# Level products of a gated recurrence: one fp32 matmul per product against three fp32r matmuls on rounded halves, with half of the tokens moving

## The chip, the cores and the metric

The kernel runs on one core of a Trainium2 chip. The metric is the device time of one execution in microseconds, as the median of the runs shown. TensorE (PE in the profile) multiplies, and its weight loads have records of their own (PEld); VectorE is DVE, ScalarE is ACT, GpSimd is POOL, and SP issues most of the DMAs.

## The reference, cut to what matters

Two blocks of two layers each work on 256 tokens of width 2048. Nearly all of the arithmetic is in the projections. The change is in the first layer of the first block, in a gated recurrence with 8 heads of 128 channels:

```python
def hgrn2_chunkwise(q, logf, k, v):
    ...
    bcum = jnp.cumsum(lc, axis=3)
    causal = jnp.tril(jnp.ones((B_CHUNK, B_CHUNK), dtype=bool))
    pair = jnp.exp(jnp.minimum(bcum[:, :, :, :, None, :] - bcum[:, :, :, None, :, :], 0.0))
    att = jnp.einsum('bhnik,bhnjk,bhnijk->bhnij', qc, kc, pair)
    att = jnp.where(causal, att, 0.0)
    o_intra = jnp.einsum('bhnij,bhnjv->bhniv', att, vc)
    ...
    o = o_intra + o_inter
```

Over the whole sequence this is an attention matrix between tokens i and j <= i: the sum over the 128 channels of q_i * k_j * exp(sum of logf from j+1 to i), times v.

## The kernel before

**Projections.** Weights come from HBM as `raw` tiles of 128x1024 floats (SP issues the loads, line 205). ACT rounds a tile to `whi` (fp32r, `split_hi`, line 217) and DVE makes the rest `wlo = raw - whi` (`split_lo`, line 235). A product of activations and weights is then three fp32r matmuls, high by high, high by low, low by high, into one PSUM tile `ps` (`mm_step`, line 1234). A pair of one raw tile's halves is a piece; there are 804 pieces, up to 5 `whi` and 4 `wlo` tiles are alive at once, and each engine takes its instructions in the order in which they are written.

A piece of a chunk in mode "x" is 12 matmuls with 512 moving columns of weights and the activations as stationary operand; in mode "w" it is 24 matmuls with 256 moving columns of tokens and the weights stationary.

**Work between the pieces.** After each piece `pump` takes one step of the first generator in `pri` and one of the first three in `bg`, and `ahead` writes the splits of later pieces. So what a generator writes between two `yield`s comes to stand between two pieces on every engine.

**The levels.** `levels(hf)` (line 726) handles 4 heads, and runs twice. It builds the attention matrix by levels: at level l (0 to 6) the 256 tokens are cut into blocks of 2m tokens with m = 2^l, and each later half of a block meets the earlier half of the same block. `expo(l)` makes exp factors on ACT, one instruction for the later halves, one for the earlier. `factors(l, E)` updates the running sums `S` and `fb` and multiplies q into the later halves and k into the earlier halves of `E`, four DVE instructions. `products(l, E)` multiplies, for each head and each of the two blocks b of 128 tokens, the 128 columns of `E` by themselves (`mm`, recorded as line 133) into a PSUM bank `lv`, one bank for each b, and DVE copies the entries that a mask in `cl` selects into the matrix `Ad[b]` (line 768). Level 7 multiplies the first 128 tokens by the second 128, 4 products, and ACT copies them to `Ax`. In one loop turn `expo(l)` stands in one step, `factors(l)` and `products(l-1)` in the next, so two pieces of the projections lie between one level's products and the next.

The tiles `E` (128x1024) come from a pool of 11 pages, in which q, k and the running sums also live.

Of the kernel before, what the change touches and what calls it, by code (L numbers as in the profile page):

```python
# [10 lines left out]
F32 = mybir.dt.float32  # L11
# [14 lines left out]

# persistent constants
C_ID, C_ONE, C_GTT, C_LT, C_LE, C_LET, C_COS, C_SIN = 0, 128, 256, 384, 512, 640, 768, 832
C_W = 896
# constants of the even layer, then of the two modulated layers  # L30
L_W = 1024
# [68 lines left out]
def two_stacks_kernel(ctx: ExitStack, tc: tile.TileContext, A, out, layers="EODM"):  # L100
# [25 lines left out]
    def bank(n="bk"):  # L126
        return p_pb.tile([128, 512], F32, tag="b", name=n)
# [4 lines left out]
    def mm(o, l, r, start=True, stop=True, **k):  # L132
        PE.matmul(o, l, r, start=start, stop=stop, skip_group_check=True, **k)  # L133
# [20 lines left out]

    # ------------------------------------------------------------------ persistent data
    x = p_c.tile([128, 2, D], F32, name="x")
# [36 lines left out]

    # ------------------------------------------------------------------ weight stream
    units = deque()     # split / mod units in order
    raws = deque()      # raw loads in order, not yet issued
    live_raw = [0]
# [53 lines left out]

    # ------------------------------------------------------------------ modulation
    mod_acc = {}
# [14 lines left out]
    def mod_fin(key):  # L268
        """column sums of the partial products, plus the bias, to a row in DRAM"""
        (i, p), col = key  # L270
        acc = mod_acc.pop(key)
        c0 = p * D + col * 512
        r = t2("mrow")
        G.dma_start(r[0:1, :], A["mod_b_2"][i, c0:c0 + 512].unsqueeze(0))
        nw = None
        if p == 1:
            nw = t2("mnw")
            G.dma_start(nw[0:1, :], A["norm_w_2"][i, col * 512:(col + 1) * 512].unsqueeze(0))
        hi, lo = t2("mhi", F32R), t2("mlo", F32R)
        yield  # L280
        act(hi, acc, AF.Copy)
        yield
        V.tensor_sub(lo, acc, hi.bitcast(F32))
        yield
        yield
        bk = bank("mb")
        mm(bk[0:1, :], cr[:, 0:1], hi, stop=False)
        mm(bk[0:1, :], cr[:, 0:1], lo, start=False)
        tt(r[0:1, :], r[0:1, :], bk[0:1, :], ADD)
        if p == 1:  # L290
            yield
            stt(r[0:1, :], r[0:1, :], 1.0, nw[0:1, :], ADD, MUL)
        if col == 0:
            mod_row[i, p] = p_dr.tile([D], F32, name=f"mod{i}{p}")
        G.dma_start(mod_row[i, p][col * 512:(col + 1) * 512].unsqueeze(0), r[0:1, :])
# [14 lines left out]

    # ------------------------------------------------------------------ silu
    def silu_gen(ps, dst, after=None):
# [19 lines left out]

    # ------------------------------------------------------------------ norm at a layer's start
    class Norm:
# [80 lines left out]

    # ------------------------------------------------------------------ y^T
    yt = [Act()]
# [22 lines left out]
    def yS_gen(pg, q, gate=None):  # L440
        """split of a page [feat, 4 K-chunks, tok]"""
        Y = yt[0]
        yield
        while gate is not None and not gate():
            yield
        Y.hi[q] = hi = act32r("yhi")
        lo = act32r("ylo")
        src = pg.rearrange("p (k t) -> p k t", k=4)
        act(hi, src, AF.Copy)
        yield  # L450
        V.tensor_sub(lo, src, hi.bitcast(F32))
        Y.lo[q] = lo

    # ------------------------------------------------------------------ evacuations
    def v3(ps):
        return ps.rearrange("p (b f) -> p b f", b=2)

    def ev_T(ps, scale, dst):
        """[feat, head, tok] of 4 heads"""
        t = page("qkT")  # L460
        act(t, ps, AF.Copy, scale=scale)
        dst.append(t.rearrange("p (h t) -> p h t", h=4))
        yield
# [20 lines left out]

    # ------------------------------------------------------------------ layer E
    def layer_E():
# [8 lines left out]
        lbt = ms[:, 280:288]  # L495
        colA = ms[:, 288:296]      # log max(lb, floor)
        colC = ms[:, 296:304]      # log1p(-lb)
        colCA = ms[:, 304:312]
        col1 = ms[:, 312:320]      # 1 - lb
        colk = ms[:, 320:328]      # lb - max(lb, floor)  # L500
        cos = cp[:, C_COS:C_COS + 64].rearrange("p (b f) -> p b f", b=2)
# [11 lines left out]
        def prepare():  # L513
            for k, (w, sc) in enumerate([(qw, 0.125), (kw, 1.0)]):
# [8 lines left out]
                tabs.append((Ct, St))  # L523
            # softmax over the single even row, then cumsum minus the first row
            tt(lb, lbt, lbt, SUB)
# [13 lines left out]
        def rope(src, H, tab, outp):  # L539
            """src: PSUM view [128, 2, H*64]; writes outp [128, 2, H, 64] (normed, rotated)."""  # L540
            Ct, St = tab
# [134 lines left out]

        # ---- B
        def ev_f(ps, hf):
# [47 lines left out]
        def levels(hf):  # L726
# [33 lines left out]

            def products(l, E):
                if l < 7:
                    for b in range(2):
                        bk = bank("lv")
                        w = slice(b * 128, (b + 1) * 128)
                        for h in range(4):
                            mm(bk[:, h * 128:(h + 1) * 128], h4(E)[:, h, w], h4(E)[:, h, w])
                        V.copy_predicated(
                            h4(Ad[b]),
                            cl[:, None, l * 128:(l + 1) * 128].bitcast(I32).to_broadcast([128, 4, 128]), h4(bk))  # L770
                else:
                    bk = bank("lv")
                    for h in range(4):
                        mm(bk[:, h * 128:(h + 1) * 128], h4(E)[:, h, 0:128], h4(E)[:, h, 128:256])
                    act(Ax, bk, AF.Copy)
# [5 lines left out]
            yield  # L781
            for l in range(1, 8):
                En = expo(l)
                yield
                factors(l, En)
                products(l - 1, E)
                E = En
                yield
            del En
            yield  # L790
            products(7, E)
            del E, Sp, Pp, q, k
            while ("bi", hf) not in st:
# [48 lines left out]

    # ------------------------------------------------------------------ layer O
    def layer_O():
# [78 lines left out]

    # ------------------------------------------------------------------ layers D and M
    def layer_DM(which):
# [14 lines left out]
        def head(st, tri, g, h):  # L940
# [3 lines left out]
            g_ = g if which == "D" else 3  # L944
            dm = cl_h[0][:, g_ * 256:g_ * 256 + 256]     # the second block of queries; its right half is also the first
            sp = bank("s")
# [5 lines left out]
            yield  # L952
            m = sm("mD")       # 0:2 -max, 2:4 sums, 4:6 alpha, 8:10 -max so far, 10:12 denominator so far
            V.tensor_reduce(m[:, 0:1], s[:, 0:128], axis=AX.X, op=MAX, negate=True)
# [100 lines left out]

    # ------------------------------------------------------------------ plan
    def out_chunks(w, gate, nxt):
# [63 lines left out]
    def make_pieces(c, order=(0, 1, 2, 3)):  # L1121
        """raw loads and pieces of a chunk; the quarters of K in the given order"""
        wv = c.w.rearrange("(k p) n -> p k n", p=128)
        rk = 2 if c.n == 512 else 4
        for q in order:
            for r0 in range(q * 4, q * 4 + 4, rk):
                r = Raw("w", wv[:, r0:r0 + rk, c.c0:c.c0 + c.n], rk, c.n)
                r.left = 1
                c.pieces.append(Piece(r, 0, rk, c.n, r0))
        c.k_first, c.k_last = c.pieces[0].kc0, c.pieces[-1].kc0 + c.pieces[-1].nk - 1  # L1130
        return c.pieces
# [14 lines left out]
    with tc.manual_schedule():  # L1146
# [7 lines left out]

        # the plan of all layers: chunks in order, with the modulation matvec spread between
        plans = []
        norms = [norm_of[l]() for l in layers] + [norm_of["F"]()]
        for li, l in enumerate(layers):
# [7 lines left out]
            ws += po[0][:6] + po[1][:6] + po[0][6:] + po[1][6:] + po[2] + po[3] + po[4]  # L1166
            # the modulation's loads, spread evenly over a stretch of the layer
            w0, w1 = (len(ws) - 68, len(ws) - 12) if l == "E" else (16, len(ws) - 40)
# [39 lines left out]
        def norm_x(b):  # L1208
            """of the first layer: 1/rms on the diagonal of a matrix that transposes x"""
            for c0 in range(0, D, 512):  # L1210
                norm.squares(b, c0, 512)
            norm.rstd(b)
            d = t2("diag")[:, 0:128]
            ts(d, ident, norm.r[b], None, MUL)
            return d
# [49 lines left out]
        for li, (l, ch, setup, oc, po) in enumerate(plans):  # L1265
# [55 lines left out]

            # ---- output projection
            final[0] = li == len(plans) - 1
# [83 lines left out]
```

## Time and profile before

| | us |
|---|---|
| median of the 3 runs | 2548.24 (2547.06 to 2548.41) |
| profiled execution, from its first to its last instruction | 2546.2 |
| PE busy in it | 2511.9 |
| DVE busy | 1708.4 |
| ACT busy | 1225.4 |

The page gives the profiled execution's own time as its span; the timed median is 2.0 us above it, which is what lies around a span. Busy times of one engine count an instruction from its start to its end, with overlaps counted once. A matmul's record begins where it starts and ends some way behind the start of the next, because matmuls are pipelined: what one costs is read from the distance of starts or from the chain of work, not from its duration. An fp32 matmul leaves two records (and two weight loads), an fp32r matmul one.

### The profile page before, as it was taken

Reading aid. Unit: us, or ns where it says so; the run is one execution under the profiler, and the core shown is the slowest. Engines: PE = TensorE matmul, PEld = TensorE weight load, DVE = VectorE, ACT = ScalarE, POOL = GpSimd, SP = SyncE. Lnnn points to the kernel's source line nnn. Section 1 sums busy time; section 2 is a strip of 40 time slices with the busy share of each in tenths; the row PEclk is TensorE's granted clock in tenths of the full one; section 3 lists DMA queues with packets and bytes.
Section 4 is the critical chain, followed back from the end, with each engine's and each line's share of the span. In section 5 each row is a group of like instructions: output and inputs, shape, how many; then the busy total and the mean of one; then the engine's idle time right before and its main releaser. Section 6 shows DMA issues by size and latency. Waiting matters only on the chain.

```text
span 2546.2 us, 42808 instructions
## 1 busy us (share of the span) xinstructions
PE 2511.9 (99%) x17140; PEld 2334.2 (92%) x17140; DVE 1708.4 (67%) x2423; ACT 1225.4 (48%) x1747; POOL 86.7 (3%) x134
## 2 busy tenths in 40 slices
PE   7999999999999999999999999999999999999998
PEld 7898888999999989999999999989998899999987
DVE  5687866588888655566666666676566656676565
ACT  5555554454554544444444444444444444444443
POOL 1000200000000000000000000000000010000000
PEclk9999999999999999999999999999999999999999
DMA  7645435588878656666666676667666656766763
GB/s 233 182 134 172 151 131 190 167 269 286 270 267 281 207 167 202 222 229 225 228 224 220 222 239 219 220 225 238 221 225 203 204 159 220 240 214 221 232 202 110
DMA packets 293496, 539.36 MB, mean 212 GB/s; under 512 B 18784, under 2 KB 49664, under 8 KB 293296
## 3 DMA queue, kind: packets, MB, share of 16 engines
q1 hardware_dynamic: 288720, 527.97, 63.4%
q0 software_dynamic: 4576, 8.66, 1.4%
q8 instruction: 134, 2.20, 0.3%
q14 instruction: 66, 0.54, 0.1%
HBM read 534.41 MB, written 2.15 MB: 211 GB/s over the span
## 4 chain that ended last, share of the span: by engine, by line
PE 97%; DVE 1%; issue 1%; ACT 1%; DMA 0%; POOL 0%; POOLq 0%; ACTq 0%; DVEq 0%
PE ps L133 88%; PE oD L133 2%; PE s L133 2%; PE lv L133 1%; PE pT L136 1%; PE mb L133 0%; PE z L133 0%; PE oO L133 0%; PE oA L133 0%; DVE wlo L235 0%; PE rc L133 0%; PE hT L133 0%; DVE hlo L414 0%; ACT junk L139 0%; PE hT L136 0%
## 5 line engine op out<-in xcount | busy, mean ns | idle before, releaser
L235 DVE TENSOR_TENSOR wlo<-raw,whi 128x1024 fp32r<-128x1024 f32 x804 | 985.7, 1227 | 558.8 <-PE ps L133 281.4
L139 ACT ACTIVATE whi<-raw 128x1024 fp32r<-128x1024 f32 x804 | 849.3, 1059 | 951.1 <-PE ps L133 838.8
L133 PE MATMUL ps<-hhi,whi 128*128 128x256 f32 x3328 | 949.4, 285 | 0.0
L133 PE MATMUL ps<-hhi,wlo 128*128 128x256 f32 x3328 | 941.6, 283 | 0.0
L133 PE MATMUL ps<-hlo,whi 128*128 128x256 f32 x3328 | 941.5, 283 | 0.0
L133 PEld LDWEIGHTS ps<-hhi,whi 128*128 128x128 f32 x3328 | 638.3, 192 | 2.1 <-issue 1.4
L133 PEld LDWEIGHTS ps<-hlo,whi 128*128 128x128 f32 x3328 | 638.4, 192 | 1.2
L133 PEld LDWEIGHTS ps<-hhi,wlo 128*128 128x128 f32 x3328 | 638.1, 192 | 0.0
L133 PE MATMUL ps<-whi,hhi 128*128 128x512 f32 (+1 forms) x1152 | 437.1, 379 | 0.0
L133 PE MATMUL ps<-whi,hlo 128*128 128x512 f32 (+1 forms) x1152 | 427.8, 371 | 1.4 <-DVE hlo L414 1.1
L133 PE MATMUL ps<-wlo,hhi 128*128 128x512 f32 (+1 forms) x1152 | 426.2, 370 | 0.1
L151 DVE SCALAR_TENSOR_TENSOR macc<-raw,cs,macc 128x512 f32<-128x512 f32 x360 | 268.2, 745 | 0.6
L133 PEld LDWEIGHTS ps<-whi,hlo 128*128 128x128 f32 x1152 | 218.0, 189 | 40.8 <-DVE hlo L414 3.2
L133 PEld LDWEIGHTS ps<-whi,hhi 128*128 128x128 f32 x1152 | 218.5, 190 | 35.0 <-issue 1.1
L133 PEld LDWEIGHTS ps<-wlo,hhi 128*128 128x128 f32 x1152 | 218.6, 190 | 34.3 <-DVE wlo L235 0.3
L133 PE MATMUL ps<-whi,yhi 128*128 128x512 f32 (+1 forms) x640 | 224.5, 351 | 2.1 <-DVE gx L142 1.0
L133 PE MATMUL ps<-whi,ylo 128*128 128x512 f32 (+1 forms) x640 | 222.1, 347 | 0.0
L133 PE MATMUL ps<-wlo,yhi 128*128 128x512 f32 (+1 forms) x640 | 221.9, 347 | 0.0
L133 PEld LDWEIGHTS ps<-whi,yhi 128*128 128x128 f32 x640 | 121.2, 189 | 17.4 <-DVE gx L142 1.4
L133 PEld LDWEIGHTS ps<-whi,ylo 128*128 128x128 f32 x640 | 121.1, 189 | 15.2
L133 PEld LDWEIGHTS ps<-wlo,yhi 128*128 128x128 f32 x640 | 121.2, 189 | 14.7
L151 DVE SCALAR_TENSOR_TENSOR sD<-cld,s 128x128 f32<-128x128 f32 (+1 forms) x128 | 39.5, 350 | 55.2 <-PE s L133 54.1
(216 smaller groups left out, 1575.2 us busy)
## 6 DMA issues: line engine op xcount, KB each, us to landing
raw<-in_a_w_in_dram SPq DMA_DIRECT2D x320, 512.0 KB, 3.7
raw<-in_mod_w_dram SPq DMA_DIRECT2D x192, 512.0 KB, 4.5
raw<-in_w_in_odd_dram SPq DMA_DIRECT2D x128, 512.0 KB, 4.0
raw<-in_b_w_in_dram SPq DMA_DIRECT2D x128, 512.0 KB, 3.9
raw<-in_w_in_even_dram SPq DMA_DIRECT2D x100, 512.0 KB, 4.1
raw<-in_w_out_even_dram SPq DMA_DIRECT2D x32, 512.0 KB, 4.4
raw<-in_w_out_odd_dram SPq DMA_DIRECT2D x32, 512.0 KB, 4.3
raw<-in_a_w_out_dram SPq DMA_DIRECT2D x32, 512.0 KB, 4.6
```

The lines of the kernel that those rows point to most:

```text
L133: PE.matmul(o, l, r, start=start, stop=stop, skip_group_check=True, **k)
L136: PE.transpose(o, i, ident)
L139: S.activation(o, i, f, **k)
L151: V.scalar_tensor_tensor(o, a, s, b, op0=op0, op1=op1)
L235: V.tensor_sub(u.lo, u.raw.t[:, u.k0 * u.n:(u.k0 + u.nk) * u.n], u.hi.bitcast(F32))
```

## The change

The products are no longer fp32. `halves(E)` makes a rounded page `Eh` (ACT) and the rest `El = E - Eh` (DVE), both fp32r. `three` multiplies high by high, high by low and low by high into the same columns of PSUM. For levels 0 to 6 only the later half of each block moves (64 columns of the 128, with steps of 2m), since the mask lets nothing else through; the results of both b lie in one bank, and the masked copy takes 256 instead of 512 columns for each b. Level 7 keeps its 128 moving columns and becomes three matmuls too. Comments were dropped elsewhere in the file, and nothing else differs.

```diff
-            def products(l, E):
+            def halves(E):
+                Eh = p_pg.tile([128, 1024], F32R, tag="pg", name="Eh")
+                act(Eh, E, AF.Copy)
+                El = p_pg.tile([128, 1024], F32R, tag="pg", name="El")
+                V.tensor_sub(El, E, Eh.bitcast(F32))
+                return h4(Eh), h4(El)
+
+            def three(o, hi, lo, h, w, sel):
+                mm(o, hi[:, h, w], sel(hi), stop=False)
+                mm(o, hi[:, h, w], sel(lo), start=False, stop=False)
+                mm(o, lo[:, h, w], sel(hi), start=False)
+
+            def products(l, E2):
+                hi, lo = E2
                 if l < 7:
+                    m = 1 << l
+                    bk = bank("lv")
+                    second = lambda a: a.rearrange("p (n z m) -> p n z m", z=2, m=m)[:, :, 1, :]
                     for b in range(2):
-                        bk = bank("lv")
                         w = slice(b * 128, (b + 1) * 128)
                         for h in range(4):
-                            mm(bk[:, h * 128:(h + 1) * 128], h4(E)[:, h, w], h4(E)[:, h, w])
+                            o = bk[:, (b * 4 + h) * 64:(b * 4 + h + 1) * 64]
+                            three(o.rearrange("p (n m) -> p n m", m=m), hi, lo, h, w, lambda a: second(a[:, h, w]))
+                    for b in range(2):
                         V.copy_predicated(
-                            h4(Ad[b]),
-                            cl[:, None, l * 128:(l + 1) * 128].bitcast(I32).to_broadcast([128, 4, 128]), h4(bk))
+                            Ad[b].rearrange("p (h n z m) -> p h n z m", h=4, z=2, m=m)[:, :, :, 1, :],
+                            second(cl[:, l * 128:(l + 1) * 128].bitcast(I32))[:, None].to_broadcast([128, 4, 64 // m, m]),
+                            bk[:, b * 256:b * 256 + 256].rearrange("p (h n m) -> p h n m", h=4, m=m))
                 else:
                     bk = bank("lv")
                     for h in range(4):
-                        mm(bk[:, h * 128:(h + 1) * 128], h4(E)[:, h, 0:128], h4(E)[:, h, 128:256])
+                        three(bk[:, h * 128:(h + 1) * 128], hi, lo, h, slice(0, 128), lambda a: a[:, h, 128:256])
                     act(Ax, bk, AF.Copy)
...
             for l in range(1, 8):
+                E2 = halves(E)
+                del E
                 En = expo(l)
                 yield
                 factors(l, En)
-                products(l - 1, E)
+                products(l - 1, E2)
                 E = En
+                del En, E2
                 yield
-            del En
-            yield
-            products(7, E)
-            del E, Sp, Pp, q, k
+            E2 = halves(E)
+            del E
+            yield
+            products(7, E2)
+            del E2, Sp, Pp, q, k
```

On PE, before, a level's products stand as 8 fp32 matmuls between two pieces; here the first level of the first half of the heads.

```order
 L133 MATMUL ps<-wlo,hhi 128x512
 L133 MATMUL ps<-whi,hlo 128x512
-L133 MATMUL lv<-E 128x128 x8
-L133 MATMUL ps<-whi,hhi 128x512
-L133 MATMUL ps<-wlo,hhi 128x512
```

On PE, after, at the same place: `Eh` and `El` are the two rounded halves of `E`. Two products are shown, of the eight.

```order
+L133 MATMUL lv<-Eh 128x64
+L133 MATMUL lv<-El,Eh 128x64
+L133 MATMUL lv<-Eh,El 128x64
+L133 MATMUL lv<-Eh 128x64
+L133 MATMUL lv<-El,Eh 128x64
+L133 MATMUL lv<-Eh,El 128x64
```

The place between the pieces stays; what was 8 instructions is 24 with half of the moving columns.

On DVE, one level's stretch with its differences, at level 1 of the first half of the heads: `A_1091` and `A_1092` are the matrices of the two blocks of tokens.

```order
-L235 TENSOR_TENSOR wlo<-raw,whi 128x1024 x2
+L235 TENSOR_TENSOR wlo<-raw,whi 128x1024
+L766 TENSOR_TENSOR El<-E,Eh 128x1024
+L235 TENSOR_TENSOR wlo<-raw,whi 128x1024
 L142 TENSOR_TENSOR S<-S,fb 128x128x4
 L142 TENSOR_TENSOR fb<-fb 128x128x4
 L142 TENSOR_TENSOR E<-E,bq 128x128x4
 L142 TENSOR_TENSOR E<-E,fn 128x128x4
-L768 COPY_PREDICATED A_1091<-cl,lv 128x512
-L768 COPY_PREDICATED A_1092<-cl,lv 128x512
+L787 COPY_PREDICATED A_1091<-cl,lv 128x128x2
+L787 COPY_PREDICATED A_1092<-cl,lv 128x128x2
```

The subtraction that makes `El` stands between the two weight splits of the level, ahead of the next level's factors, and the two masked copies are half as wide.

On ACT, the same stretch.

```order
 L139 ACTIVATE whi<-raw 128x1024 x2
+L139 ACTIVATE Eh<-E 128x1024
 L139 ACTIVATE E<-fb 128x256x2
 L139 ACTIVATE E<-S 128x256x2
 L139 ACTIVATE whi<-raw 128x1024 x2
+L139 ACTIVATE Eh<-E 128x1024
```

The rounding copy comes behind two weight splits and ahead of the next level's two exponentials.

## Rows read from the trace of the kernel before

**Rows 1.** The page of the profiled execution: busy times of the engines with their shares of the span and their instructions, and the chain of work that ended last, by engine and by line.

```profile
PE 2511.9 (99%) x17140; PEld 2334.2 (92%) x17140; DVE 1708.4 (67%) x2423; ACT 1225.4 (48%) x1747; POOL 86.7 (3%) x134
...
PE 97%; DVE 1%; issue 1%; ACT 1%; DMA 0%; POOL 0%; POOLq 0%; ACTq 0%; DVEq 0%
PE ps L133 88%; PE oD L133 2%; PE s L133 2%; PE lv L133 1%; PE pT L136 1%; PE mb L133 0%; PE z L133 0%; PE oO L133 0%; PE oA L133 0%; DVE wlo L235 0%; PE rc L133 0%; PE hT L133 0%; DVE hlo L414 0%; ACT junk L139 0%; PE hT L136 0%
```

**Rows 2.** The chain of work that ended last, from 100 to 300 us, in order of time: start, length, engine, tile, and how many records are merged. The stretch holds both passes of the levels.

```profile
120.45 1.78 PE lv L133 x16
122.24 5.46 PE ps L133 x24
...
142.63 1.79 PE lv L133 x16
144.41 5.75 PE ps L133 x48
...
172.79 0.89 PE lv L133 x8
...
279.55 0.89 PE lv L133 x8
```

**Rows 3.** The instructions on the tile `lv`: count, duration in ns (least, median, greatest), first and last start, and their form.

```profile
L133 PE MATMUL lv<-E x240: 270/275/275, 120.3 to 280.2; 128*128 128x128 f32 x120
L768 DVE COPY_PREDICATED A<-cl,lv x28: 722/750/765, 121.4 to 274.1; 128x512 f32<-128x512 int32 x28
```

**Rows 4.** TensorE's instructions by form, line 133: an fp32 product with 64 moving columns; and under it, from the chain of 300 to 400 us, two runs of such records.

```profile
L133 PE MATMUL oA<-va,pT 128*128 128x64 f32 x96 | 11.2, 272 | 0.0
...
320.71 2.62 PE oA L133 x24
...
357.90 3.96 PE oA L133 x36
```

**Rows 5.** TensorE's weight loads by line: two of the three loads of a product of a w-mode piece, whose stationary operand `whi` is the same for both.

```profile
L133 PEld LDWEIGHTS ps<-hhi,whi 128*128 128x128 f32 x3328 | 638.3, 192 | 2.1 <-issue 1.4
L133 PEld LDWEIGHTS ps<-hlo,whi 128*128 128x128 f32 x3328 | 638.4, 192 | 1.2
```

**Rows 6.** The timeline of 554.3 to 556.2 us, the starts of matmuls: fp32r products of `rc` (384 and 128 moving columns), and the pieces behind them.

```profile
554.87 0.22 PE L133 MATMUL rc<-onh,cr 128*128 128x128 f32 x1
554.93 0.27 PE L133 MATMUL rc<-onl,cr 128*128 128x128 f32 x1
555.04 0.39 PE L133 MATMUL rc<-onh,cr 128*128 128x384 f32 x1
555.27 0.34 PE L133 MATMUL rc<-onl,cr 128*128 128x384 f32 x1
555.44 0.22 PE L133 MATMUL rc<-onh,cr 128*128 128x128 f32 x1
555.50 0.27 PE L133 MATMUL rc<-onl,cr 128*128 128x128 f32 x1
555.61 0.34 PE L133 MATMUL ps<-hhi,whi 128*128 128x256 f32 x1
555.78 0.28 PE L133 MATMUL ps<-hlo,whi 128*128 128x256 f32 x1
```

**Rows 7.** Weight loads of fp32r operands, of 128 columns (`rc`) and of a single column (`mb`): count, duration in ns (least, median, greatest), first and last start, form.

```profile
L133 PEld LDWEIGHTS rc<-onl,cr x32: 187/188/192, 554.5 to 867.4; 128*128 128x128 f32 x32
L133 PEld LDWEIGHTS mb<-mhi,cr x24: 82/86/86, 558.4 to 2418.4; 128*1 128x1 f32 x24
```

**Rows 8.** DVE in the timeline, one level of the first pass with the extra work of another generator: start, length, instruction.

```profile
148.52 0.68 DVE L142 TENSOR_TENSOR S<-S,fb 128x512 f32<-128x512 f32 x1
...
151.10 1.64 DVE L768 COPY_PREDICATED A<-cl,lv 128x512 f32<-128x512 int32 x2
152.63 1.22 DVE L235 TENSOR_TENSOR wlo<-raw,whi 128x1024 fp32r<-128x1024 f32 x1
153.75 1.22 DVE L142 TENSOR_TENSOR bg<-bg,ps 128x1024 f32<-128x1024 f32 x1
155.01 1.22 DVE L142 TENSOR_TENSOR bg<-bg,emisc 128x1024 f32<-128x1024 f32 x1
156.15 1.22 DVE L235 TENSOR_TENSOR wlo<-raw,whi 128x1024 fp32r<-128x1024 f32 x1
157.28 0.68 DVE L142 TENSOR_TENSOR S<-S,fb 128x512 f32<-128x512 f32 x1
```

**Rows 9.** Products of DVE with 512 and 256 elements, by line, and ACT's copies of 1024 elements in the first pass: busy us, mean ns, idle time before them.

```profile
L142 DVE TENSOR_TENSOR E<-E,bq 128x512 f32<-128x512 f32 x16 | 11.0, 685 | 0.0
L142 DVE TENSOR_TENSOR yD<-oD,sg 128x256 f32<-128x256 f32 x16 | 6.8, 424 | 16.4 <-PE oD L133 16.4
L139 ACT ACTIVATE whi<-raw 128x1024 fp32r<-128x1024 f32 x14 | 14.8, 1059 | 25.2 <-PE ps L133 16.2 <-issue 7.3 <-ACT fa L139 0.9
```

**Rows 10.** Windows: length, busy us of PE, PEld, DVE, ACT and POOL with the instructions begun in each, the granted clock, and the DMA engines' share and GB/s. One window near the kernel's start, the first and the last part of the first pass, and one run of the 64-column products.

```profile
20.00:31.00 11.00, 10.73 (x70) 10.73 (x71) 6.71 (x23) 6.33 (x19) 0.13 (x1) 0.73 0.89 330
120.30:134.90 14.60, 14.60 (x93) 13.17 (x92) 12.79 (x17) 7.24 (x9) 0.00 (x0) 1.00 0.52 146
149.90:173.50 23.60, 23.60 (x204) 23.60 (x202) 19.04 (x24) 11.35 (x13) 0.00 (x0) 1.00 0.49 144
357.70:361.70 4.00, 4.00 (x38) 3.96 (x37) 3.96 (x7) 1.06 (x1) 0.00 (x0) 1.00 0.76 240
```

## Prediction

> **What bounds the kernel now.** I read the page first: PE is busy for 2511.9 of 2546.2 us and holds 97% of the chain that ended last, 88% of it in the projections' `ps`, while the level products `lv` are 1% [rows 1]. DVE and ACT are busy for 67% and 48%, so they matter only where a PE instruction needs what they make. Next the chain in the stretch of the change. It is PE without a gap: two pieces of projections (5.46 us in x-mode, 5.75 us in w-mode), one level's products (1.78 or 1.79 us), two pieces, and so on; level 7 takes 0.89 us [rows 2]. A microsecond that the products take more or less is therefore one of the whole time, as long as DVE keeps up. All products together: 14 x 1.785 + 2 x 0.89 = 26.8 us, for 240 records [rows 3], so 0.112 us a record.
>
> **What sets those 0.112 us.** This is the number on which the forecast hangs. An fp32 product with half of the moving columns, 64 in `oA`, takes 2.62 / 24 = 0.109 and 3.96 / 36 = 0.110 us a record [rows 4], the same as `lv` with 128. So the moving columns are not what is paid for. Each record goes with a weight load. A load of 128 columns takes 188 ns and one of a single column 86 ns, both fp32r [rows 7]: 127 columns more cost 102 ns, which is nearly the whole 0.11 us. I read the price of a small matmul as the price of loading 128 columns of weights, for fp32 and fp32r alike.
>
> For small fp32r products the trace has only `rc`. Its 384-column products start 0.17 us apart (555.27 to 555.44). The 128-column ones show both sides: 0.06 us after 554.87, where the weights had been loaded under a long product, then 0.11 us to 555.04. One head costs 555.61 - 555.04 = 0.57 us; less 2 x 0.173 for its long products, 0.224 is left for two short ones, 0.112 each [rows 6]. And a load is not saved where the next matmul has the same stationary operand: in w-mode `whi` serves two matmuls in a row, and both have their 3328 loads [rows 5].
>
> **The change on PE.** It removes 240 records at 0.112 us (26.8 us). It adds 14 x 24 matmuls with 64 columns and 2 x 12 with 128, 360 in all, each with its load. The price is bounded below by `rc`'s 0.06 (load hidden) and above by a w-mode matmul with 256 columns, 5.75 / 48 = 0.120 us [rows 2]. I take 0.111, between `oA`'s 0.110 and `rc`'s 0.112, the rows nearest in columns and in type: 360 x 0.111 = 40.0 us. The difference is **+13.2 us**. Half of the moving columns buys nothing, and three loads replace two. With 0.100 (a stream of loads at the bare 102 ns) it would be about +9.2 us, with 0.120 +16.4 us. The moving operand now has steps of up to two elements between columns; no row shows that on PE, and it could cost only from the point where 64 columns take over 0.11 us, so I take nothing.
>
> The rule that speaks for the change is in the Trainium skill, FP8 and Floating Point Precision, section Matmul Precision: true fp32 makes four passes through the array. By it a product would go from 4 x 128 to 3 x 64 column steps, and PE would gain. The `oA` rows speak against it: there the columns were halved and the time stayed [rows 4]. What it would give is the first rival below.
>
> **The change on DVE and ACT.** ACT gets 16 copies `Eh` of 1.06 us. They stand where ACT sits idle for 25.2 us of a pass [rows 9], and are done while PE is at its two pieces, so they cost nothing; without that cover it would be 17 us. DVE gets 16 subtractions `El`, 1.13 us from start to start like the weight split of the same shape, and its 28 masked copies lose 256 of 512 elements, 685 - 424 = 0.26 us each [rows 8, 9]. A level before: factors 2.58 (148.52 to 151.10), copies 1.53, two weight splits 2.26, together 6.4 us. After: 2.58 + 1.01 + 3.39 = 7.0 us. PE's period grows from 7.24 to 5.46 + 24 x 0.111 = 8.1 us (x-mode) or 8.4 us (w-mode), so DVE stays the shorter.
>
> One bank for both blocks has a price too. The first masked copy now waits for all 24 matmuls; queued behind it on DVE are a weight split and `El`, and the next products wait for `El`. From the end of a level's products: 0.2 (wait) + 1.0 + 1.13 + 1.13 = 3.5 us until `El` is done, and PE asks for it after 5.46 us. That hides it, with 2 us to spare. Where the gate's generator puts two more products of 1.2 us between (153.75 and 155.01 [rows 8]), and the level before already had one, `El` is late by up to about 0.5 us, once in each pass, more likely in the second with its shorter x-mode pieces. I take **+0.5 us** in all, with bounds 0 and 2. The page reuse makes the next exponentials wait for the products that read the old halves; these end two pieces earlier than the exponentials are needed, and what queues behind on ACT are weight splits several pieces ahead: nothing. DMAs are unchanged.
>
> **The sum.** 2546.2 + 13.2 + 0.5 = 2559.9 us of span; with the 2.0 us between the span and the median of the runs shown, **2562 us**, 0.54% slower. Its own range goes from 0.100 without a stall (2557) to 0.120 with 2 us (2567).
>
> **The rivals.** A measurement of this kernel can tell about 0.2%, 5.1 us, from no change: below 2543.1 is faster, above 2553.3 slower.
>
> *Loads hidden, not slower.* If every small fp32r matmul cost the 0.06 us of `rc`'s hidden load [rows 6], the products would take 21.6 us: 2543 by PE alone. It decides from 26.8 / 360 = 0.074 us downwards. For it: that one distance. Against it: the 0.11 right behind it. And PE's period would be 6.9 us in x-mode, while DVE needs 7.0 plus the gate's 3.5 us in a pass, so `El` would become the bound and give part back: 2543 to 2551, likeliest 2547. Chance 0.10, half of it under 2543.
>
> *Loads partly hidden.* With a price midway between 0.06 and 0.10, 0.08 us, the products take 28.8 us: +2.0, 2550. It would need a load to begin earlier before the end of the matmul ahead than in `rc`. Chance 0.04. The Trainium skill, TensorE: Matmul & The Clock Gate, section Back-to-back issue gap, gives about 81 ns for pairs of load and matmul with 128 columns, though not for fp32r; by that figure the estimate is 29.2 us, +2.4. No row here comes down to it except after a long product.
>
> *`El` late at every level.* DVE takes all its instructions in order. If its copies with small strides cost twice the price, or ACT's rounding came late behind a weight split, PE would wait at every level; at 1 us each that is 14 us more, 2576. It begins where DVE's part before `El` grows by over 2 us. Against it: the four factors have all strides from 1 to 64 and one price, 685 ns [rows 9]. Chance 0.05.
>
> *The clock.* If the narrow matmuls lowered the granted clock and the next piece ran at 1.2 instead of 2.4 GHz, 14 x 2.73 = 38 us more, 2600. The clock was at 0.73 of full speed in 20 to 31 us, near the start; it stayed at 1.00 through all of `lv` and through 4 us of `oA` with 64 columns [rows 10]. Chance 0.02.
>
> **How the numbers follow.** The forecast has 0.79. The range 2556 to 2568 is its own, widened by 1 us at each end; the rivals outside hold 0.21. Slower: 0.79 + 0.05 + 0.02 and 0.01 of the first rival, 0.87. Same: 0.04 of the first and 0.04 of the second, 0.08. Faster: 0.05.
>
> **What would show it.** In the profile after: 360 records of `lv`, in blocks of 24 that hold 2.6 to 2.7 us of the chain, starts 0.11 us apart, with no difference between the 64 columns of levels 0 to 6 and the 128 of level 7 (12 records, 1.3 us); pieces between them unchanged at 5.46 and 5.75; `ps` with the same total; at most one wait of PE for `El` in each pass, under 1 us. Masked copies near 0.49 us, `El` near 1.22 and `Eh` near 1.06 us. Starts of 0.06 us would prove me wrong, and so would PE idling before the second matmul of a block, or a granted clock below 1.00 between 120 and 300 us.

## The result, and the profile after

The median of 4 runs is 2560.8 us (2560.66 to 2562.27), against 2548.22 us of the kernel before (4 runs): slower by 0.53%, ratio 1.0053 with a 95% interval of 1.0039 to 1.0066. The forecast was 2562 us.

The page of the changed kernel, busy times and the chain that ended last (compare [rows 1]):

```profile
PE 2526.4 (99%) x17260; PEld 2348.7 (92%) x17260; DVE 1718.4 (67%) x2439; ACT 1242.1 (49%) x1763; POOL 86.7 (3%) x134
...
PE 97%; DVE 1%; issue 1%; ACT 1%; DMA 0%; POOL 0%; POOLq 0%; ACTq 0%; SPq 0%; DVEq 0%
```

PE has 120 records and loads more and is busy for 14.5 us longer; it holds the same 97% of the chain. The time went into the levels. The granted clock was 1.00 from 100 to 310 us. The chain there, in order of time (start, length, merged records), beside [rows 2]:

```profile
119.55 2.61 PE lv L133 x24
122.16 5.54 PE ps L133 x24
...
144.43 2.60 PE lv L133 x24
147.03 5.83 PE ps L133 x48
...
178.16 1.29 PE lv L133 x12
...
269.87 5.55 PE ps L133 x24
275.42 2.71 PE lv L133 x24
```

A level's products hold 2.60 us where they held 1.78, and the two pieces behind them 0.08 us more. That 0.08 is a matter of where the chain draws the line: it books a block until its last record ends, which is now 0.17 us behind the next matmul's start (121.87 + 0.28 against 121.98) and was 0.25 us before (120.29 + 1.95 against 121.99, shown below). So the price is read from one block to the next: it is 8.15 us in x-mode and 8.43 us in w-mode, against 7.24 and 7.54. So a block costs 8.15 - 5.46 = 2.69 us, 0.112 us for each of its 24 matmuls. The starts on PE show it directly, at the head and at the end of the first block:

```profile
119.39 0.22 PE L133 MATMUL lv<-Eh 128*128 128x64 f32 x1
119.43 0.27 PE L133 MATMUL lv<-El,Eh 128*128 128x64 f32 x1
...
121.65 0.28 PE L133 MATMUL lv<-Eh 128*128 128x64 f32 x1
121.76 0.28 PE L133 MATMUL lv<-El,Eh 128*128 128x64 f32 x1
121.87 0.28 PE L133 MATMUL lv<-Eh,El 128*128 128x64 f32 x1
121.98 0.48 PE L133 MATMUL ps<-whi,hhi 128*128 128x512 f32 x1
122.30 0.40 PE L133 MATMUL ps<-wlo,hhi 128*128 128x512 f32 x1
```

They are 0.11 us apart for 64 moving columns, but for the second of a block, which comes 0.04 us after the first; from the long matmul behind the block to the next it is 0.32 us instead of 0.23. Both are in the 2.69 us. The same place in the kernel before, with its 16 records merged:

```profile
120.29 1.95 PE L133 MATMUL lv<-E 128*128 128x128 f32 x16
121.99 0.48 PE L133 MATMUL ps<-whi,hhi 128*128 128x512 f32 x1
```

Level 7, with 128 moving columns, takes 1.29 us for 12, and 0.06 us more go into the piece behind it: 0.112 us each, the same price.

The whole kernel also varies by 1.3 to 1.6 us from run to run, and part of that lies where the change does nothing: the first `dg` product, ahead of the levels, starts between 106.6 and 108.0 us in the traces of the nine kernels. To leave that out I use a stretch: from the first `dg` product, just ahead of the levels, to the first `rc` product of the second layer. Both are in the views of the two tiles (count, durations in ns, first and last start), first of the kernel before, then of the changed one:

```profile
L133 PE MATMUL dg<-bq,fn x32: 270/275/275, 107.6 to 217.7; 128*128 128x128 f32 x32
...
L133 PE MATMUL rc<-onh,cr x32: 222/278/391, 554.5 to 867.4; 128*128 128x384 f32 x16, 128*128 128x128 f32 x16
```

```profile
L133 PE MATMUL dg<-bq,fn x32: 270/275/275, 106.7 to 223.5; 128*128 128x128 f32 x32
...
L133 PE MATMUL rc<-onh,cr x32: 221/278/391, 567.3 to 880.2; 128*128 128x384 f32 x16, 128*128 128x128 f32 x16
```

The stretch grows from 446.9 to 460.6 us, by **13.7 us**. That is the sum that was worked out for the change (13.2 + 0.5), but to the tenth it is luck: the part on PE came out 0.4 us larger and the wait 0.3 to 0.4 us smaller, as shown further down.

### The profile page after: what moved, and what is told of

It reads as the page before. It is cut to its first block, busy times and chain, and to the rows that moved or that the text cites. A ratio compares the mean times of both kernels' runs of the same rounds, so it can differ in the third digit from the quotient of the medians.

```text
span 2560.5 us, 43070 instructions
## 1 busy us (share of the span) xinstructions
PE 2526.4 (99%) x17260; PEld 2348.7 (92%) x17260; DVE 1718.4 (67%) x2439; ACT 1242.1 (49%) x1763; POOL 86.7 (3%) x134
## 4 chain that ended last, share of the span: by engine, by line
PE 97%; DVE 1%; issue 1%; ACT 1%; DMA 0%; POOL 0%; POOLq 0%; ACTq 0%; SPq 0%; DVEq 0%
PE ps L133 87%; PE oD L133 2%; PE s L133 2%; PE lv L133 2%; PE pT L136 1%; PE mb L133 0%; PE z L133 0%; PE oO L133 0%; PE oA L133 0%; DVE wlo L235 0%; PE rc L133 0%; DVE hlo L414 0%; PE hT L136 0%; PE hT L133 0%; PE yT L136 0%
```

## The experiments

Theory L is that of the prediction: a small matmul costs the load of its 128 stationary columns, so the count of loads decides. Four rivals were set against it: the moving columns (M), a fixed price for each record whatever it loads (F), the work added on DVE and ACT (C), and the adding into the same PSUM columns by three matmuls in a row (A). The stretch is read from one trace of each kernel; among the three kernels whose products stay fp32 with full loads it differs by 0.2 us.

| kernel | loads | median us | against before, 95% interval | stretch us |
|---|---|---|---|---|
| before | 240 | 2548.2 | | 446.9 |
| changed | 360 | 2560.8 | 1.0039 to 1.0066 | 460.6 |
| all columns move | 360 | 2561.9 | 1.0042 to 1.0069 | 461.1 |
| fp32, half the columns move | 240 | 2548.4 | 0.9993 to 1.0011 | 447.1 |
| two matmuls | 240 | 2549.3 | 0.9995 to 1.0014 | 447.7 |
| halves unused | 240 | 2548.1 | 0.9991 to 1.0009 | 447.0 |
| changed, 64 columns loaded | 336 narrow, 24 full | 2546.5 | 0.9987 to 1.0004 | 444.8 |
| fp32, 64 columns loaded | 224 narrow, 16 full | 2540.0 | 0.9959 to 0.9982 | 439.8 |
| one rounded matmul | 120 | 2534.6 | 0.9933 to 0.9958 | 433.6 |

### The moving columns alone, in both directions

First the changed kernel with all columns moving.

```diff
-    o = bk[:, (b * 4 + h) * 64:(b * 4 + h + 1) * 64]
-    three(o.rearrange("p (n m) -> p n m", m=m), hi, lo, h, w, lambda a: second(a[:, h, w]))
+    three(bk[:, h * 128:(h + 1) * 128], hi, lo, h, w, lambda a: a[:, h, w])
...
```

> The changed kernel with all 128 columns moving again in levels 0 to 6, one bank and full masked copies for each block of tokens, as before the change; the three matmuls on halves stay. Theory L (a small matmul costs the load of its 128 stationary columns, 0.112 us): 360 loads as in the changed kernel, so 2561 us, within 1.5 us of the changed kernel, and blocks of 24 records at 2.6 us. Rival M (the moving columns are paid): 336 x 64 columns more at 2.4 GHz, 336 x 0.027 = 9 us more, 2570 us.

The chain and the products' forms:

```profile
119.46 2.63 PE lv L133 x24
122.09 5.55 PE ps L133 x24
```

```profile
L133 PE MATMUL lv<-Eh x120: 220/274/277, 119.3 to 293.0; 128*128 128x128 f32 x120
```

2561.9 us, with blocks of 2.63 us for twice the moving columns. Then the same halving alone, in the fp32 kernel.

```diff
-    mm(bk[:, h * 128:(h + 1) * 128], h4(E)[:, h, w], h4(E)[:, h, w])
+    o = bk[:, (b * 4 + h) * 64:(b * 4 + h + 1) * 64]
+    mm(o.rearrange("p (n m) -> p n m", m=m), h4(E)[:, h, w], second(h4(E)[:, h, w]))
...
```

> The kernel before, fp32, one matmul per product, with only the later halves moving, one bank and half copies: the other part of the change alone. Theory L: 240 records and loads as before, 2548 us, blocks of 16 records at 1.78 us. Rival M: the block of a level falls by half, 14 x 0.89 = 12.5 us less, 2536 us.

```profile
120.81 1.73 PE lv L133 x16
122.54 5.54 PE ps L133 x24
```

```profile
L133 PE MATMUL lv<-E x240: 217/275/275, 120.6 to 280.7; 128*128 128x64 f32 x112, 128*128 128x128 f32 x8
```

2548.4 us: 1.73 + 0.08 us a block, what it was with 128 columns. M falls in fp32r and in fp32: the half of the change that halves the moving columns is worth nothing on PE. So the reckoning in column steps that spoke for the change, 4 x 128 against 3 x 64, does not give the time of these products.

### The work added on DVE and ACT

```diff
+                E2 = halves(E)
                 En = expo(l)
                 yield
                 factors(l, En)
                 products(l - 1, E)
...
```

> The kernel before with the two halves made at each level, as in the change, and not used: the products stay fp32. Theory L (the change is paid on PE alone, the extra copies of ACT and subtractions of DVE lie beside other work): 2548 to 2550 us. Rival C (the change is paid on DVE or ACT): 16 x 1.22 us of DVE, or 16 x 1.06 of ACT, are on the path at least in part: over 2555 us.

2548.1 us, no difference. The window of the first pass (length, busy PE, PEld, DVE, ACT and POOL with instructions, granted clock, DMA):

```profile
120.30:173.50 53.20, 53.20 (x422) 51.77 (x421) 52.35 (x64) 34.73 (x42) 0.00 (x0) 1.00 0.48 140
```

DVE is busy for 52.35 of 53.20 us there, and PE is still busy for all of it. So the added work as such costs nothing, and C falls in that sense. But no product of this kernel reads the halves, so it can't show what a late `El` would cost. That is read from the changed kernel, where among all waits from 100 to 310 us a load of the products waits for `El` once:

```profile
PEld lv L133 <- DVE El L766: 0.2, 1, 0.2
```

The kernel with unused halves also shows how little cover is left: its copies are still of full width, and DVE is full.

### The size of a load

```diff
+def thin(o, hi, lo, h, w, m, sel):
+    first = lambda a: a[:, h, w.start:w.start + 64]
+    mm(o, first(hi), sel(hi), stop=False)
+    mm(o, first(hi), sel(lo), start=False, stop=False)
+    mm(o, first(lo), sel(hi), start=False)
...
-    three(o.rearrange("p (n m) -> p n m", m=m), hi, lo, h, w, lambda a: second(a[:, h, w]))
+    thin(o[0:64].rearrange("p (n m) -> p n m", m=m), hi, lo, h, w, m, lambda a: second(a[:, h, w]))
...
```

> The changed kernel with 64 instead of 128 stationary columns in levels 0 to 6 (the first 64 of a block, so the level products are not the reference's); the count of matmuls, their 64 moving columns and the three steps are unchanged, the masked copies take 64 partitions. Theory L: the load of 64 columns costs 64 x 0.80 = 51 ns less (188 against 86 ns for 128 columns and one), so 0.061 us a matmul: 336 x 0.061 + 24 x 0.112 = 23.2 instead of 40.3 us, 2543.6 us by PE alone; PE's period would be 6.9 us in x-mode against 7.0 of DVE, so PE should begin to wait for the low halves, and the time lies between 2544 and 2549 us. Rival F (a fixed price of 0.11 us for each record, whatever it loads) and rival M: 2561 us, unchanged.

Same count of matmuls, same moving columns, half of the stationary ones. Loads of the tile, and then the starts of one block:

```profile
L133 PEld LDWEIGHTS lv<-El,Eh x120: 133/138/192, 119.3 to 276.8; 128*64 128x64 f32 x112, 128*128 128x128 f32 x8
```

```profile
120.55 0.25 PE L133 MATMUL lv<-Eh 128*64 128x64 f32 x1
120.61 0.25 PE L133 MATMUL lv<-El,Eh 128*64 128x64 f32 x1
120.67 0.25 PE L133 MATMUL lv<-Eh,El 128*64 128x64 f32 x1
120.72 0.47 PE L133 MATMUL ps<-whi,hhi 128*128 128x512 f32 x1
```

A load of 64 columns takes 138 instead of 192 ns, and the starts fall from 0.11 to 0.06 us, 0.059 on the mean of the block (119.31 to 120.72 for 24). The stretch is 15.8 us shorter than the changed kernel's. F falls, and this is the run that carries theory L: the price goes with the stationary columns. Fewer of them also mean an output of 64 instead of 128 partitions, and no run separates that from the load; what speaks for the load is that its own record shortens by the 54 ns by which the starts come closer (53 ns). The run also brought the other side that was expected. The chain leaves PE here:

```profile
122.17 1.09 issue
123.26 1.19 DVE El L766
124.45 1.13 DVE wlo L235
```

From 116 to 155 us, and again in the second pass, it runs over DVE: PE is the faster engine and waits for the low halves. An undisturbed block adds 1.44 to 1.49 us to the pieces around it, 0.060 to 0.062 us a matmul. By that PE alone would gain 3.3 to 3.9 us on the kernel before (26.8 - 336 x 0.062 - 24 x 0.112, and the same with 0.060); the stretch gains 2.1, so 1.2 to 1.8 us go back to DVE, by this estimate.

The same in fp32, where there are no halves to wait for; the edit is shown against the fp32 kernel with half of the columns moving:

```diff
-    mm(o.rearrange("p (n m) -> p n m", m=m), h4(E)[:, h, w], second(h4(E)[:, h, w]))
+    mm(o[0:64].rearrange("p (n m) -> p n m", m=m), h4(E)[:, h, w.start:w.start + 64], second(h4(E)[:, h, w]))
...
```

> The kernel before, fp32, with the later halves moving and with 64 instead of 128 stationary columns in levels 0 to 6 (the first 64 of a block, so the level products are not the reference's). Theory L: fp32 records pay their load too, 224 x 0.062 + 16 x 0.112 = 15.7 instead of 26.8 us: 2537 us; there are no halves to wait for, DVE needs about 5.9 us of a period of 6.5, so nothing is given back, unlike in the changed kernel with 64 stationary columns (2546.5 us). Rival F (each record has a fixed price): 2548 us.

2540.0 us, faster than before as L says and F does not, but 3 us above the 2537 I expected. The chain, and the starts around a block:

```profile
120.56 1.08 PE lv L133 x16
121.64 5.67 PE ps L133 x24
```

```profile
120.18 0.39 PE L133 MATMUL ps<-whi,hlo 128*128 128x512 f32 x1
120.49 1.15 PE L133 MATMUL lv<-E 128*64 128x64 f32 x16
121.57 0.50 PE L133 MATMUL ps<-whi,hhi 128*128 128x512 f32 x1
121.91 0.39 PE L133 MATMUL ps<-wlo,hhi 128*128 128x512 f32 x1
```

```profile
120.49 1.01 PEld L133 LDWEIGHTS lv<-E 128*64 128x64 f32 x16 [0.35 <-DVE fb L142]
```

A block costs 1.08 us inside, 0.068 a record, and its head is dearer: 0.31 us from the last long matmul to the first record where the others have 0.23, because the first load begins only at 120.49; behind the block it is 0.34 us where the others have 0.32. With the pieces behind it (5.67 against 5.46) that is 1.08 + 0.20 = 1.28 us instead of the 0.99 I had taken, 4 us over 14 blocks. In the stretch that is the miss: 7.1 us shorter than before, where 11.1 were expected. Why the first load of a narrow fp32 block does not begin under the matmul ahead of it, as it does with fp32r, is left open.

### The count of loads

Two matmuls instead of three:

```diff
     mm(o, hi[:, h, w], sel(hi), stop=False)
-    mm(o, hi[:, h, w], sel(lo), start=False, stop=False)
-    mm(o, lo[:, h, w], sel(hi), start=False)
+    mm(o, hi[:, h, w], sel(lo), start=False)
```

> The changed kernel without the third matmul of each product (low half stationary, high half moving is left out). Theory L: 240 loads of 128 columns, as many as the 240 records before the change, 26.9 us: 2548 us, with up to 2 us for late low halves, since PE's period falls back to 7.2 to 7.5 us against 7.0 of DVE. Rival A (what costs 0.11 us is that matmuls add into the same columns of PSUM one right behind the other): 120 first matmuls of a product are free of it, so the starts would alternate between under 0.07 and over 0.11 us.

```profile
119.57 1.71 PE lv L133 x16
121.29 5.54 PE ps L133 x24
```

2549.3 us. 16 fp32r matmuls take 1.71 + 0.08 us, what 16 fp32 records took. Their starts do not alternate:

```profile
120.00 0.28 PE L133 MATMUL lv<-Eh 128*128 128x64 f32 x1
120.11 0.28 PE L133 MATMUL lv<-El,Eh 128*128 128x64 f32 x1
120.22 0.28 PE L133 MATMUL lv<-Eh 128*128 128x64 f32 x1
```

A matmul that begins a product comes 0.11 us behind the one ahead of it, just as one that adds to it does. The stretch is 0.8 us longer than before; in the second pass the chain passes over DVE again, as expected with a shorter PE period.

And one matmul, with `E` rounded by the factors' own output:

```diff
-    tt(vE[:, :, 1, :], vE[:, :, 1, :], vw(q, m)[:, :, 1, :], MUL)
-    tt(vE[:, :, 0, :], vE[:, :, 0, :], vw(k, m)[:, :, 0, :], MUL)
+    Er = p_pg.tile([128, 1024], F32R, tag="pg", name="Er")
+    vR = vw(Er, m)
+    tt(vR[:, :, 1, :], vE[:, :, 1, :], vw(q, m)[:, :, 1, :], MUL)
+    tt(vR[:, :, 0, :], vE[:, :, 0, :], vw(k, m)[:, :, 0, :], MUL)
+    return Er
...
-    mm(bk[:, h * 128:(h + 1) * 128], h4(E)[:, h, w], h4(E)[:, h, w])
+    mm(o.rearrange("p (n m) -> p n m", m=m), h4(E)[:, h, w], second(h4(E)[:, h, w]))
```

> One fp32r matmul per product: the factors write E rounded to fp32r, no halves are made, and the two matmuls with low halves are left out, so q, k and their decays are multiplied at fp32r's precision; only the later halves move. Theory L: 120 loads, 120 x 0.112 = 13.4 us instead of 26.8 of the kernel before: 2535 us, starts 0.11 us apart. Rival A (adding into the same columns): starts under 0.07 us, 2530 us or less.

```profile
120.64 0.82 PE lv L133 x8
121.46 5.54 PE ps L133 x24
```

2534.6 us, 0.54% under the kernel before; 0.82 + 0.08 us for 8 matmuls, again 0.112 each, although none of them adds to what another has written. A falls here too. With 120, 240 and 360 loads of full width the stretch is 433.6, 446.9 to 447.7 and 460.6 to 461.1 us: 13 to 14 us for every 120 loads, where 120 x 0.112 gives 13.4. This version beats both kernels, at the price of fp32r's precision in the level products; whether that may be paid is not a matter of the time.

## Why the prediction was right

**The price of a small matmul.** This was the step on which all hung, and it held: 0.111 us taken, 0.112 measured. It goes with the load: only fewer loads (one or two matmuls a product) or narrower ones (64 columns) changed the time, and the moving columns, the added work, the count of records by itself and the adding in PSUM did not. That the load, and not the narrower output, makes the difference at 64 columns is argued from the load's record and not tested by itself. The reading from `oA` [rows 4], where fp32 with 64 moving columns costs what 128 do, carried over to fp32r. The slope read from two load durations [rows 7], 0.80 ns a column, was 0.84 by the loads of 64 and 128 columns (54 ns) and 0.83 by the starts (0.112 against 0.059 us for 64 columns less). The Trainium skill, TensorE: Matmul & The Clock Gate, section LDWEIGHTS (loading the stationary operand), gives columns divided by 1.2 as the time in ns, 0.83 a column; the slope in these runs agrees, while a load's own record of 128 columns lasts 192 ns, longer than the 107 ns that this gives.

**The sum on PE.** 13.2 us forecast; 13.6 by the blocks (14 x (2.69 - 1.785) + 2 x (1.29 + 0.06 - 0.89), the 0.06 being what the piece behind level 7 is longer). The halved moving columns bought nothing, as said, and their steps of two elements cost nothing that can be seen: level 0 has the same 2.61 us as the rest, and the kernel with all columns moving is no faster.

**The cover of DVE and ACT.** It held for the changed kernel, though one term of it was not the same at all levels. From the first masked copy of a pair to the instruction behind it I took 1.01 us, after 1.53; it was 0.67 us at levels 2 to 6 and 1.13 to 1.15 us at levels 0 and 1 (last section), and `El` was not late there either. `El` took 1217 ns and `Eh` 1057 ns. The one place where I expected a late `El` is there: two gate products ahead of it in the second pass.

```profile
269.91 0.78 DVE L787 COPY_PREDICATED A<-cl,lv 128x256 f32<-128x256 int32 x2 [0.32 <-PE lv L133]
270.58 1.21 DVE L235 TENSOR_TENSOR wlo<-raw,whi 128x1024 fp32r<-128x1024 f32 x1
271.71 1.21 DVE L142 TENSOR_TENSOR bg<-bg,ps 128x1024 f32<-128x1024 f32 x1
272.96 1.22 DVE L142 TENSOR_TENSOR bg<-bg,emisc 128x1024 f32<-128x1024 f32 x1
274.10 1.22 DVE L766 TENSOR_TENSOR El<-E,Eh 128x1024 fp32r<-128x1024 f32 x1
```

`El` ends at 275.32 us, when PE had just asked for it, and the block of 2.71 us in the chain above is the one that waited. That cost 0.1 to 0.2 us in all, not the 0.5 I took: the halved copies of that level were cheaper than I had them (0.67 us, 269.91 to 270.58), and in the first pass nothing waited. So the forecast of 13.7 us holds two errors in size, 13.2 for 13.6 and 0.5 for 0.1 to 0.2, that cancel.

**The rivals.** Hidden and partly hidden loads did not come. The second matmul of a block, behind a long one as in `rc`, does start sooner than the sign in the prediction allows, 0.03 or 0.04 us after the first with 64 moving columns and 0.06 us with the 128 of level 7 (but not in the block that waited for `El`). The time is made up for at the block's end, and all others are 0.10 to 0.11 us apart; a stream of starts at 0.06 us came only with 64 loaded columns. `El` was not late at every level, though copies with small strides were indeed dearer, at two levels of seven. The granted clock of the changed kernel was 1.00 in the window from 100 to 310 us. The claim that DVE would become the bound if PE got faster, which was part of the first rival, was right in the run with 64 loaded columns.

**The total.** 2562 against 2560.8. The span came out as 2560.5 us in the profiled execution, where I had 2559.9. What is left lies within the 1.3 to 1.6 us by which runs of one kernel differ, so the total alone would not tell 13.2 from 13.7; the stretch and the starts do.

## What to carry to other kernels

For matmuls with few moving columns on 4-byte operands, count the weight loads, not the moving columns: here each cost 0.112 us for 128 stationary columns, whether the matmul behind it was an fp32 record or fp32r and had 64 or 128 columns. So three fp32r matmuls on rounded halves cost half as much again as one fp32 matmul, which leaves two records. Before the moving side of a small product is narrowed, see whether the stationary side can be.

## What the runs showed of the hardware that I had not expected

A masked copy at the two smallest steps is dearer than the others. At level 0, where it takes every second element, and at level 1, where it takes pairs, the two copies of 256 elements took 1.33 or 1.34 us together; at levels 2 to 6 they took 0.77 or 0.78 us. The first three levels of the first pass:

```profile
122.19 1.33 DVE L787 COPY_PREDICATED A<-cl,lv 128x256 f32<-128x256 int32 x2 [1.11 <-PE lv L133]
130.34 1.33 DVE L787 COPY_PREDICATED A<-cl,lv 128x256 f32<-128x256 int32 x2 [0.96 <-PE lv L133]
138.64 0.77 DVE L787 COPY_PREDICATED A<-cl,lv 128x256 f32<-128x256 int32 x2 [1.12 <-PE lv L133]
```

To the start of the instruction behind them it is 1.13 to 1.15 us at levels 0 and 1 and 0.67 us at the others, where two copies of 512 elements had 1.53 us before [rows 8]. The products of DVE over the same steps showed no such thing (681 to 691 ns in the changed kernel, over all levels). And a narrow fp32 block has a dearer head than a narrow fp32r block, 0.31 against 0.23 us, with a cause that stays open.
